# The second product of q and k over all 128 partitions in three attentions

## The chip, the cores and the metric

The kernel runs as one program on one core of a Trainium2 chip. The metric is the device time of one execution in microseconds (us), from the runs of the kernel; a profiled execution beside them gives the trace. A core has five engines that work side by side, each through its own queue in order: TensorE (PE in the rows; its weight loads are listed apart as PEld), VectorE (DVE), ScalarE (ACT), GpSimd (POOL) and SyncE (SP), which issues DMAs. Lines such as L1123 are lines of the kernel before.

## What is computed

Two blocks follow each other on 512 tokens of width 1024, in float32. The first is a hybrid layer: a state-space branch, an attention over a sliding window with sinks, and a mixture of 64 experts. The second puts 16 learned tokens in front (528 rows) and runs two layers, one with a stick-breaking attention and one with a differential attention, each followed by an MLP. Cut to the three products that matter here:

```
scores = einsum('bnqhgd,bnkhd->bnhgqk', qb, kk) * ATT_SCALE      # sliding window: 16 heads of 64, 4 of k
z = einsum('bhqd,bhkd->bhqk', qb, kf) * scale                    # stick-breaking: 16 heads of 64
s = einsum('bhqd,bhkd->bhqk', qb, kk) * scale                    # differential: 8 heads, two q and two k of 64 each
```

In all three the length that is summed over is 64, half of the 128 partitions.

## The kernel before, in words

Matrix products run in a fast format that keeps fewer bits than float32. To keep the accuracy, an operand is split in two: a first part (the rounded value, made by ScalarE with a copy into that format) and a second part (what is left, made by VectorE or GpSimd with a subtraction). A product of two split matrices is then three products that are added into one sum in PSUM: first by first, first by second, second by first (`mm3s`, whose products go through `mm`, L229; where the order of TensorE is pinned to the order of the program they show as L242).

In the attentions the head's length of 64 leaves half of the partitions free, and the kernel uses them: a tile `qs` holds q's first part on 64 partitions and q's second part on the other 64, and `ks` holds k's first part twice. One product of `qs` with `ks` over 128 partitions thus makes two of the three products. The third, q's first part with k's second part `kl`, is made over the 64 partitions on which q's first part stands.

- Sliding window (`swa_qk`, L1080; `swa_scores`, L1107): k of each of the 4 groups stands twice on the partitions already (`kd`, L1049), so `ks` and `kl` are both 128 partitions high. For each group and each of 4 blocks of 128 tokens there are 4 pairs of products, L1122 and L1123, of 256 columns. The steps of this attention are woven with projections of the state-space branch (`dense_x`, `dense_z`), which fill TensorE.
- Stick-breaking (`sb_split`, L1807; `sb_scores`, L1886): two heads share one `kl` tile, the even head on partitions 0 to 63, the odd one on 64 to 127. For each of 16 heads there are products of 512, 384, 256 and 256 columns, L1897 and L1898. Here the order on TensorE is that of the program (`in_order`, L232); `sb_steps` (L1834) writes the stages of the attention out step by step, with the projections of the next heads (`qkv`, L1772) and later of the output (`out_early`, L1738) woven in. `sb_soft` (L1909) and `sb_weights` (L1918) are the work behind the scores: two clippings, exponential, logarithm, and a scan along the keys on VectorE, a subtraction on GpSimd (L1925), an exponential on ScalarE (L1926).
- Differential (`diff_split`, L2341; `diff_scores`, L2355): one `dkl` tile per head holds both second parts, one on each half. For each of 8 heads and 4 blocks of tokens there are 2 pairs of products, and 2 more in the last block; 272, 256, 400, and 256 with 272 columns, L2372 and L2373. The fills are the projections of q, k, v of the later heads and the output projection.

The tiles of these attentions come from pools: `self.la` with tag `qk` (7 buffers) in layer A; the general helper `self.S`, with 34 slots in the second block, in layer B. Which instruction stands where on an engine other than a pinned one is decided by the framework's scheduler; waits and buffer addresses are its work too.

Of the kernel before, what the change touches and what calls it, by code (L numbers as in the profile page):

```python
# [64 lines left out]
class K:  # L65
# [1041 lines left out]
    def swa_scores(self, S, kv, n, mask, snk):  # L1107
        nc, sm = self.nc, self.sm
        k0 = 0 if n else 128
        nk = 256 - k0  # L1110
        x0 = max(n - 1, 0) * 128
        qs = slice(n * 128, (n + 1) * 128)
        ks, kl, qq = S
        pp = []
        for par in range(2):
            p = self.P()
            pp.append(p)
            a = slice(64 * par, 64 * par + 64)
            for i in range(2):
                q = qq[2 * i + par]  # L1120
                o = p[:, i * 256:i * 256 + 256]
                nc.tensor.matmul(o, lhsT=q[:, qs], rhs=ks[:, x0:x0 + 256], start=True, stop=False)  # L1122
                nc.tensor.matmul(o, lhsT=q[a, qs], rhs=kl[a, x0:x0 + 256], start=False, stop=True)  # L1123
        sc = []
        mx = sm.tile([128, 4], F32, tag="mx", bufs=3, name="mx")
        sums = sm.tile([128, 4], F32, tag="sums", bufs=3, name="sums")
        for par in range(2):
            s = self.S(name="sc")
            sv = s[:, :512].rearrange("p (i k) -> p i k", i=2)
            pv = pp[par].rearrange("p (i k) -> p i k", i=2)  # L1130
            for i in range(2):
                nc.vector.tensor_tensor_reduce(sv[:, i, :nk], pv[:, i, :nk], mask[:, k0:], 1.0, NEG, op0=ALU.add, op1=ALU.max, accum_out=mx[:, par * 2 + i:par * 2 + i + 1])
            sc.append(sv)
        sk = snk[:, 4 * kv:4 * kv + 4].rearrange("p (i a) -> p a i", a=2)
        mx2 = mx.rearrange("p (a i) -> p a i", a=2)
        nm = sm.tile([128, 4], F32, tag="nm", bufs=3, name="nm")
        nc.vector.tensor_tensor(mx2, mx2, sk, op=ALU.max)
        es = sm.tile([128, 4], F32, tag="es", bufs=3, name="es")
        nc.vector.tensor_tensor(es.rearrange("p (a i) -> p a i", a=2), sk, mx2, op=ALU.subtract)
        nc.vector.tensor_scalar(nm, mx, -1.0, None, op0=ALU.mult)  # L1140
        nc.scalar.activation(es, es, AF.Exp)
        for par in range(2):
            for i in range(2):
                j = par * 2 + i
                nc.scalar.activation(sc[par][:, i, :nk], sc[par][:, i, :nk], AF.Exp, bias=nm[:, j:j + 1], accum_out=sums[:, j:j + 1])
        nc.vector.tensor_tensor(sums, sums, es, op=ALU.add)
        nc.vector.reciprocal(sums, sums)
        for par in range(2):
            for i in range(2):
                j = par * 2 + i  # L1150
                nc.gpsimd.tensor_scalar(sc[par][:, i, :nk], sc[par][:, i, :nk], sums[:, j:j + 1], None, op0=ALU.mult)
        return (sc,)
# [507 lines left out]
    def layer_a(self, hT, g, g1):  # L1660

        V = self.nc.vector
        h_d = self.H_d("h_d")
        N = self.norm_begin(g, h_d)
        for k in range(8):
            self.norm_tile(N, k, hT[k])
        xs = list(N["xs"])
        self.o_d = self.dr.tile([2, 8, 128, 528], F32, name="o_d")
        r = {}

        def late():
            r["k"], r["c"] = self.norm_end(N, self.KB)
            r["q"] = self.S(name="rq")
            V.tensor_scalar(r["q"], r["k"], 0.125, None, op0=ALU.mult)
        sets = [{"late": False} for _ in range(4)]
        W = self.I["a_w_o"]
        self.ahead([(self.I["a_w_qkv"][i + hg], 2048, 8) for hg in range(4) for i in (0, 4, 8)] + [(W[u][:, :1280], 1280, 5) for u in range(4)]
                   + [(W[u][:, 1280:], 768, 3) for u in range(4)])
        self.rest([self.qkv(0, xs, r, sets[0], late)])
        del hT, N  # L1680
        ho = {}
        heads = [(hg, j) for hg in range(4) for j in range(4)]
        with self.in_order("tensor"):
            fills = [self.qkv(hg, xs, r, sets[hg]) for hg in (1, 2, 3)]
            self.o67 = []
            self.zt = [self.zero_tail(i) for i in range(2)]
            o = [], []

            def loads(k0, k1, to=None):
                for k in range(k0, k1):  # L1690
                    for x, y in zip(o, self.load_o(k, None if to is None else to[2 * k:2 * k + 2])):
                        x.append(y)
                    yield 0.2

            def need(hg, what):
                while what not in sets[hg]:
                    if next(fills[0], None) is None:
                        fills.pop(0)

            def begin(t):  # L1700

                if t == 11:
                    raw = self.st.tile([128, 2112], F32R, tag="raw", bufs=self.NRAW, name="ohl").rearrange("p (a c) -> p a c", a=4)
                    to = [self.hp.tile([128, T2], F32R, tag="h", bufs=8, name="ohl") for _ in range(4)] + [raw[:, x] for x in range(4)]
                    fills.insert(0, loads(0, 4, to))
                if t == 12:
                    fills.insert(0, loads(4, 5))
                if t == 13:
                    self.rest(fills)
                    xs.clear()  # L1710
                    r.clear()
                    fills[:] = [self.out_early(h_d, ho, o)]
                sets[3]["late"] = t >= 14
            self.weave(self.sb_steps(sets, heads, need, begin), fills, .79)
            self.rest(fills)
        o = self.o67
        self.oT = None
        hT = [self.H8() for _ in range(8)]
        self.wide = 2
        N = self.norm_begin(g1)  # L1720
        self.rest([self.out_proj(self.I["a_w_o"], 5, 8, [x[0] for x in o], [x[1] for x in o], ho["h"], self.H, 0, hT, N)])
        self.wide = 0
        return hT, N
# [48 lines left out]
    def qkv(self, hg, xs, r, out, late=None):  # L1772
# [22 lines left out]
        for b, tl in enumerate(self.KB):  # L1795
# [8 lines left out]
                out["v"] = v  # L1804
            yield 1

    def sb_split(self, S, j):  # L1807

        nc = self.nc
        a, o = slice(64 * (j % 2), 64 * (j % 2) + 64), slice(64 - 64 * (j % 2), 128 - 64 * (j % 2))  # L1810
        q, k = S["q"][j // 2], S["k"][j // 2]
        qs, ks = [self.la.tile([128, T2], F32R, tag="qk", bufs=7, name=x) for x in ("qs", "ks")]
        if j % 2 == 0:
            S["kl"] = self.la.tile([128, T2], F32R, tag="qk", bufs=7, name="kl")
        kl = S["kl"]
        S["qk", j] = qs, ks, kl
        nc.scalar.activation(qs[a], q[a], AF.Copy)
        nc.gpsimd.tensor_tensor(qs[o], q[a], qs[a].bitcast(F32), op=ALU.subtract)
# [67 lines left out]
    def sb_scores(self, S, j, tiles):  # L1886


        lo = 64 * (j % 2)
        qs, ks, kl = S["qk", j]  # L1890
        p = self.P()
        c = 0
# [1 line left out]
        for i in tiles:  # L1894
            n, m = 128 * (i + 1), max(128 * (i + 1), 256)
            q = slice(128 * i, 128 * i + 128)
            self.mm(p[:, c:c + m], lhsT=qs[:, q], rhs=ks[:, 0:m], start=True, stop=False)  # L1897
            self.mm(p[:, c:c + m], lhsT=qs[lo:lo + 64, q], rhs=kl[lo:lo + 64, 0:m], start=False, stop=True)  # L1898
            at.append((c, c + n))
            c += n  # L1900
        x = 128 * tiles[-1] if len(tiles) == 1 else 128
# [244 lines left out]
    def layer_b(self, N, bg, kvg, g1):  # L2146
# [56 lines left out]
        def attn():  # L2203
            todo, outs = [], []
            spare = []
            for _ in range(1):
                raw = self.st.tile([128, 2112], F32R, tag="raw", bufs=self.NRAW, name="ohl").rearrange("p (a c) -> p a c", a=4)[:, :, :512]
                spare += [(raw[:, 2 * i], raw[:, 2 * i + 1]) for i in range(2)]
# [17 lines left out]
            for h in range(8):  # L2226
# [5 lines left out]
                for i in range(4):  # L2232
# [6 lines left out]
                    if len(todo) > 3:  # L2239
                        step()  # L2240
                del qk[h]
            while todo:
                step()
                yield 1.5
                norm()
# [95 lines left out]
    def diff_split(self, q, k):  # L2341

        nc = self.nc
        qs, ks = [[self.S(F32R, name=x) for _ in range(2)] for x in ("dqs", "dks")]
        kl = self.S(F32R, name="dkl")
        for m in range(2):
            a, o = slice(64 * m, 64 * m + 64), slice(64 - 64 * m, 128 - 64 * m)
            nc.scalar.activation(qs[m][a, :512], q[a], AF.Copy)
            nc.gpsimd.tensor_tensor(qs[m][o, :512], q[a], qs[m][a, :512].bitcast(F32), op=ALU.subtract)
            nc.scalar.activation(ks[m][a], k[a], AF.Copy)  # L2350
            nc.scalar.activation(ks[m][o], k[a], AF.Copy)
            nc.gpsimd.tensor_tensor(kl[a], k[a], ks[m][a].bitcast(F32), op=ALU.subtract)
        return qs, ks, kl

    def diff_scores(self, h, i, qs, ks, kl, lam):  # L2355
        nc, sm = self.nc, self.sm
# [10 lines left out]
        for x, (a, b) in enumerate(spans):  # L2367
            e = max(b, a + 256)
            for m in range(2):
                lo = 64 * m  # L2370
                p = ps[m, x] = self.P()
                self.mm(p[:, :e - a], lhsT=qs[m][:, i * 128:(i + 1) * 128], rhs=ks[m][:, a:e], start=True, stop=False)  # L2372
                self.mm(p[:, :e - a], lhsT=qs[m][lo:lo + 64, i * 128:(i + 1) * 128], rhs=kl[lo:lo + 64, a:e], start=False, stop=True)  # L2373
            for m in range(2):
                p = ps[m, x]
                if b == L:
# [154 lines left out]
```

## Time and profile before

| | |
|---|---|
| median of 3 runs | 2746.67 us (2743.1 to 2748.12) |
| profiled execution, its own time | 2747.67 us |
| its span, first to last instruction | 2745.9 us |
| mean granted clock of TensorE over the span | 0.977 |
| TensorE busy | 2605.9 us (95%), 18850 products |
| VectorE, ScalarE, GpSimd busy | 1543.9 (56%), 1090.7 (40%), 536.5 us (20%) |

The page gives shares over the whole span; the three attentions take 134, 261 and 223 us of it. A row of a table of instructions has the line, the engine, the operation, out<-in by the program's names, the shapes (for a product: weights' partitions * columns, then the moving operand's partitions x columns), the count, then busy us and mean ns of one, then idle time of the engine before them and what ended it. In a timeline the first number is the start, the second the duration. Starts of products are measured, their ends are modelled: products that follow each other overlap in the rows, so what one costs is read from start to start.

### The profile page before, as it was taken

What the parts mean: (1) busy time and instruction counts of PE and PEld (TensorE: products, weight loads), DVE (VectorE), ACT (ScalarE), POOL (GpSimd) and SP (SyncE); (2) the same over time, 40 slices, a digit from 0 to 9 for tenths busy, and PEclk for the clock granted to TensorE, in tenths of its full rate; (3) what the DMA queues carried; (4) which work ended last, traced back from release to release, by engine and by line L of the source; (5) the groups of instructions that cost most, each with busy time, mean ns of one, the idle gap of its engine ahead of it and who ended that gap; (6) DMA issues with size and microseconds to landing.
All of it is one profiled execution on the core that took longest, in us unless ns stands there. A gap on an engine that the chain in (4) does not pass through costs nothing.

```text
span 2745.9 us, 46828 instructions
## 1 busy us (share of the span) xinstructions
PE 2605.9 (95%) x18850; PEld 2197.3 (80%) x18850; DVE 1543.9 (56%) x3266; ACT 1090.7 (40%) x2249; POOL 536.5 (20%) x528
## 2 busy tenths in 40 slices
PE   7999999999989999996699999999999999999999
PEld 5986769979965555553688889999999777899999
DVE  6488556676652222221688987334467778644433
ACT  5355544433311111111467755323335666523322
POOL 0044332221111011111144430001102435100000
PEclk9999999999999999998799999999999999999999
DMA  5233255544389999994511323222231011322221
GB/s 190 87 123 110 95 182 167 178 142 169 135 363 391 419 416 393 413 413 187 201 55 32 100 80 124 90 83 90 93 128 47 32 55 47 107 86 93 93 93 62
DMA packets 111436, 436.92 MB, mean 159 GB/s; under 512 B 16505, under 2 KB 37545, under 8 KB 68976
## 3 DMA queue, kind: packets, MB, share of 16 engines
q1 hardware_dynamic: 105552, 429.20, 42.6%
q0 software_dynamic: 5520, 4.63, 0.7%
q8 instruction: 150, 2.46, 0.4%
q14 instruction: 70, 0.57, 0.1%
q10 hardware_dynamic: 144, 0.07, 0.0%
HBM read 400.52 MB, written 43.79 MB: 162 GB/s over the span
## 4 chain that ended last, share of the span: by engine, by line
PE 44%; DVE 4%; ACT 2%; issue 1%; POOL 1%; DMA 0%; SPq 0%; DVEq 0%; POOLq 0%; ACTq 0%
PE pd L229 36%; PE pd L242 3%; PE pm L242 2%; PE pm L229 1%; PE pm L2418 1%; DVE zd L1924 1%; DVE wl L180 0%; DVE zd L1913 0%; DVE zt L1912 0%; PE pm L2416 0%; DMA mraw<-y_d 0%; PE pm L2317 0%; ACT wh L179 0%; PE pm L2425 0%; PE pm L2407 0%
## 5 line engine op out<-in xcount | busy, mean ns | idle before, releaser
L229 PE MATMUL pd<-hh,wh 128*128 128x256 f32 (+2 forms) x1408 | 439.1, 313 | 12.5 <-ACT hh L209 8.8
L229 PE MATMUL pd<-hl,wh 128*128 128x256 f32 (+2 forms) x1408 | 438.8, 312 | 1.0 <-DVE hl L210 1.0
L229 PE MATMUL pd<-hh,wl 128*128 128x256 f32 (+2 forms) x1408 | 438.6, 312 | 1.0 <-DVE wl L242 1.0
L206 ACT ACTIVATE wh<-raw 128x1024 fp32r<-128x1024 f32 (+2 forms) x228 | 222.7, 1022 | 413.0 <-PE pd L229 314.2
L207 DVE TENSOR_TENSOR wl<-raw,wh 128x1024 fp32r<-128x1024 f32 (+2 forms) x228 | 281.7, 1266 | 159.4 <-ACT wh L206 159.2
L229 PEld LDWEIGHTS pd<-hh,wh 128*128 128x128 f32 x1408 | 266.9, 190 | 28.4 <-ACT hh L209 9.5
L229 PEld LDWEIGHTS pd<-hh,wl 128*128 128x128 f32 x1408 | 268.1, 191 | 16.7 <-DVE wl L242 1.9
L229 PEld LDWEIGHTS pd<-hl,wh 128*128 128x128 f32 x1408 | 267.8, 190 | 17.1 <-DVE hl L210 1.6
L229 PE MATMUL pd<-wh,hh 128*128 128x256 f32 (+2 forms) x936 | 268.7, 287 | 0.8 <-ACT tk L254 0.5
L229 PE MATMUL pd<-wl,hh 128*128 128x256 f32 (+2 forms) x936 | 264.0, 282 | 0.0
L229 PE MATMUL pd<-wh,hl 128*128 128x256 f32 (+2 forms) x936 | 263.8, 282 | 0.0
L928 PE MATMUL pd<-mraw,xg 128*48 128x256 f32 x2048 | 238.2, 386 | 0.0
L928 PEld LDWEIGHTS pd<-mraw,xg 128*48 128x48 f32 x2048 | 128.7, 124 | 90.1 <-issue 12.7
L229 PEld LDWEIGHTS pd<-wh,hh 128*128 128x128 f32 (+1 forms) x936 | 170.1, 182 | 8.7 <-issue 2.3
L229 PEld LDWEIGHTS pd<-wh,hl 128*128 128x128 f32 (+1 forms) x936 | 169.8, 181 | 2.7 <-issue 0.4
L229 PEld LDWEIGHTS pd<-wl,hh 128*128 128x128 f32 (+1 forms) x936 | 170.2, 182 | 1.9 <-issue 0.2
L898 POOL DMA_INDIRECT y_d<-ys,idx x64 | 60.5, 946 | 475.6 <-DMA y_d<-ys,idx 217.2
L229 PE MATMUL pd<-vl,wh 128*128 128x272 f32 (+1 forms) x512 | 145.3, 285 | 0.0
L229 PE MATMUL pd<-vh,wl 128*128 128x272 f32 (+1 forms) x512 | 145.2, 284 | 0.0
L229 PE MATMUL pd<-vh,wh 128*128 128x272 f32 (+1 forms) x512 | 143.8, 285 | 0.0
L229 PE MATMUL pd<-wh,vh 128*128 128x256 f32 x512 | 142.9, 281 | 0.0
L229 PE MATMUL pd<-wl,vh 128*128 128x256 f32 x512 | 142.8, 281 | 0.0
(572 smaller groups left out, 6286.6 us busy)
## 6 DMA issues: line engine op xcount, KB each, us to landing
mraw<-in_w_moe SPq DMA_DIRECT2D x192, 1024.0 KB, 15.7
raw<-in_mlp_w_in SPq DMA_DIRECT2D x32, 1024.0 KB, 4.9
raw<-in_mlp_w_out SPq DMA_DIRECT2D x32, 1024.0 KB, 4.9
raw<-in_w_xbc SPq DMA_DIRECT2D x12, 1024.0 KB, 5.2
raw<-in_a_w_qkv SPq DMA_DIRECT2D x12, 1024.0 KB, 5.4
raw<-in_w_z SPq DMA_DIRECT2D x8, 1024.0 KB, 5.1
raw<-in_w_gate_in SPq DMA_DIRECT2D x8, 1024.0 KB, 5.3
bc<-acT_d SPq DMA_DIRECT2D x32, 256.0 KB, 5.4
```

What stands on the lines that cost most here:

```text
L206: nc.scalar.activation(h, src, AF.Copy)
L207: nc.vector.tensor_tensor(l, src, h.bitcast(F32), op=ALU.subtract)
L229: self.nc.tensor.matmul(*a, **kw)
L242: return lambda *a, **kw: pin(f(*a, **kw))
L898: self.nc.gpsimd.indirect_dma_start(out=self.y_d[:, :], out_offset=bass.IndirectOffsetOnAxis(ap=rows, axis=0), in_=y[0:64 + self.CAP], in_ ...
L928: self.pin(self.nc.tensor.matmul(p[64 * i:64 * i + self.CAP, 0:256], lhsT=x[:, k], rhs=w[i][:, k], start=k == 0, stop=k == 7))
L1924: nc.vector.tensor_tensor_scan(r[0], r[1], r[0], 0.0, op0=ALU.add, op1=ALU.add)
L2418: nc.tensor.matmul(p[:, 128 * j:512], lhsT=vt[1 + j][h // 4][:, hs], rhs=self.wT[:, j, 128 * j:512], start=False, stop=j == 3)
```

## The change

The second product of each pair runs over all 128 partitions, with the whole `qs` and the whole `kl`. In the sliding window `kl` stands twice, so that product now takes in the product of the two second parts as well. In the other two, `kl` gets zeros on the partitions on which q's second part stands: in layer A two tiles `klz` from a tag of their own, one for even and one for odd heads, while the tag `qk` goes from 7 buffers to 6; in layer B four tiles from the general helper, held through the attention and used in turns of two. The zeros are written once by GpSimd (`kl_tiles`), since each tile always gets its second part on the same half.

```diff
@@ swa_scores
-            a = slice(64 * par, 64 * par + 64)
-                nc.tensor.matmul(o, lhsT=q[a, qs], rhs=kl[a, x0:x0 + 256], start=False, stop=True)
+                nc.tensor.matmul(o, lhsT=q[:, qs], rhs=kl[:, x0:x0 + 256], start=False, stop=True)
@@ layer_a
+        self.klz = self.kl_tiles([self.la.tile([128, T2], F32R, tag="kl", bufs=2, name="klz") for _ in range(2)])
+    def kl_tiles(self, kl):
+        for i, t in enumerate(kl):
+            self.nc.gpsimd.memset(t[64 - 64 * (i % 2):128 - 64 * (i % 2)].bitcast(F32), 0.0)
+        return kl
@@ sb_split
-        qs, ks = [self.la.tile([128, T2], F32R, tag="qk", bufs=7, name=x) for x in ("qs", "ks")]
-        if j % 2 == 0:
-            S["kl"] = self.la.tile([128, T2], F32R, tag="qk", bufs=7, name="kl")
-        kl = S["kl"]
+        qs, ks = [self.la.tile([128, T2], F32R, tag="qk", bufs=6, name=x) for x in ("qs", "ks")]
+        kl = self.klz[j % 2]
@@ sb_scores
-            self.mm(p[:, c:c + m], lhsT=qs[lo:lo + 64, q], rhs=kl[lo:lo + 64, 0:m], start=False, stop=True)
+            self.mm(p[:, c:c + m], lhsT=qs[:, q], rhs=kl[:, 0:m], start=False, stop=True)
@@ layer_b, attn
+            self.klz = self.kl_tiles([self.S(F32R, name="klz") for _ in range(4)])
...
+            self.klz = None
@@ diff_split
-        kl = self.S(F32R, name="dkl")
+        self.kln += 2
+        kl = self.klz[self.kln % 4:self.kln % 4 + 2]
-            nc.gpsimd.tensor_tensor(kl[a], k[a], ks[m][a].bitcast(F32), op=ALU.subtract)
+            nc.gpsimd.tensor_tensor(kl[m][a], k[a], ks[m][a].bitcast(F32), op=ALU.subtract)
@@ diff_scores
-                self.mm(p[:, :e - a], lhsT=qs[m][lo:lo + 64, i * 128:(i + 1) * 128], rhs=kl[lo:lo + 64, a:e], start=False, stop=True)
+                self.mm(p[:, :e - a], lhsT=qs[m][:, i * 128:(i + 1) * 128], rhs=kl[m][:, a:e], start=False, stop=True)
```

## Rows read from the trace of the kernel before

**Rows 1.** The page: the span, and busy time of each engine.

```profile
span 2745.9 us, 46828 instructions
...
PE 2605.9 (95%) x18850; PEld 2197.3 (80%) x18850; DVE 1543.9 (56%) x3266; ACT 1090.7 (40%) x2249; POOL 536.5 (20%) x528
```

**Rows 2.** Stretches: length; PE, PEld, DVE, ACT, POOL busy; clock; DMA share, GB/s.

```profile
231.00:365.00 134.00, 134.00 (x627) 93.33 (x627) 82.41 (x270) 72.43 (x204) 59.89 (x62) 1.00 0.25 85
1379.00:1640.00 261.00, 248.04 (x1775) 214.28 (x1774) 240.33 (x461) 180.27 (x378) 112.51 (x101) 0.99 0.21 65
2112.00:2335.00 223.00, 215.25 (x1306) 168.84 (x1305) 167.94 (x492) 139.93 (x402) 100.53 (x91) 0.95 0.13 41
...
385.00:400.00 15.00, 13.99 (x64) 10.47 (x65) 14.82 (x31) 6.50 (x11) 3.09 (x2) 0.89 0.95 324
790.00:1230.00 440.00, 415.45 (x3094) 242.79 (x3094) 120.31 (x250) 69.79 (x160) 48.30 (x51) 0.99 1.00 408
```

**Rows 3.** Groups by line and shape, PE: all products of 64x columns on kl.

```profile
L1123 PE MATMUL pm<-kl,qs 64*128 64x256 f32 x64 | 24.4, 381 | 0.0
L229 PE MATMUL pm<-dkl,dqs 64*128 64x256 f32 x32 | 12.7, 397 | 0.3 <-POOL dkl L2352 0.3
L229 PE MATMUL pm<-dkl,dqs 64*128 64x272 f32 x32 | 12.6, 395 | 0.0
L242 PE MATMUL pm<-kl,qs 64*128 64x256 f32 x32 | 12.4, 388 | 0.0
L242 PE MATMUL pm<-kl,qs 64*128 64x512 f32 x16 | 8.0, 503 | 0.0
L229 PE MATMUL pm<-dkl,dqs 64*128 64x400 f32 x16 | 7.1, 446 | 0.0
L242 PE MATMUL pm<-kl,qs 64*128 64x384 f32 x16 | 7.0, 438 | 0.0
```

**Rows 4.** Timeline of PE around the first of them: start, duration, instruction.

```profile
230.95 0.28 PE L1122 MATMUL pm<-ks,qs 128*128 128x256 f32 x1
231.16 0.38 PE L1123 MATMUL pm<-kl,qs 64*128 64x256 f32 x1
231.47 0.50 PE L229 MATMUL pd<-hh,wl 128*128 128x512 f32 x1
231.81 0.40 PE L229 MATMUL pd<-hh,wh 128*128 128x512 f32 x1
232.04 0.39 PE L229 MATMUL pd<-hl,wh 128*128 128x512 f32 x1
```

**Rows 5.** Timeline of PE around the last of them, in the differential attention.

```profile
2333.90 0.28 PE L229 MATMUL pd<-ol,wh 128*128 128x256 f32 x1
2334.02 0.29 PE L229 MATMUL pm<-dks,dqs 128*128 128x272 f32 x1
2334.24 0.39 PE L229 MATMUL pm<-dkl,dqs 64*128 64x272 f32 x1
2334.55 0.38 PE L229 MATMUL pd<-oh,wl 128*128 128x256 f32 x1
2334.78 0.40 PE L229 MATMUL pd<-ohl,wh 128*128 128x256 f32 x2
```

**Rows 6.** Timeline of the weight loads, PEld, at the first of them.

```profile
231.16 0.18 PEld L1123 LDWEIGHTS pm<-kl,qs 64*128 64x128 f32 x1 [0.25 <-issue]
...
231.58 0.19 PEld L229 LDWEIGHTS pd<-hh,wh 128*128 128x128 f32 x1
```

**Rows 7.** The chain of waits by line, 1375 to 1640 and 2110 to 2345 us.

```profile
by line: PE pd L242 25.7%; PE pm L242 20.2%; DVE zd L1924 7.8%; issue 5.5%; DVE wl L180 5.0%; DVE zd L1913 5.0%; DVE zt L1912 4.7%; PE pd L229 2.0%; POOL zs L1925 1.8%; DVE zs L1904 1.7%; ACT zs L1926 1.7%; ACT zt L1914 1.7%; ACT wh L179 1.
...
by line: PE pd L229 41.7%; PE pm L229 15.6%; PE pm L2418 9.0%; PE pm L2416 4.3%; PE pm L2407 2.6%; PE pm L2425 2.2%; ACT pr L2386 1.9%; DVE wl L210 1.7%; DVE dmx L2378 1.7%; PE pm L2317 1.4%; DVE wl L207 1.4%; ACT dks L2351 1.4%; issue 1.4%
```

**Rows 8.** POOL: memsets; a wait in 1370 to 1640 us (total, times, longest).

```profile
L666 POOL MEMSET ys<- 128x512 f32 x3 | 1.5, 530 | 0.0
...
POOL kl L1822 <- PE pm L242: 3.1, 2, 1.7
```

More of the change, by code (lines that the diff above doesn't have):

```diff
@@ L1886, in sb_scores @@
     def sb_scores(self, S, j, tiles):
-        lo = 64 * (j % 2)
         qs, ks, kl = S["qk", j]
@@ L2351, in diff_split @@
             nc.scalar.activation(ks[m][o], k[a], AF.Copy)
-            nc.gpsimd.tensor_tensor(kl[a], k[a], ks[m][a].bitcast(F32), op=ALU.subtract)
+            nc.gpsimd.tensor_tensor(kl[m][a], k[a], ks[m][a].bitcast(F32), op=ALU.subtract)
         return qs, ks, kl
+    kln = 0
     def diff_scores(self, h, i, qs, ks, kl, lam):
@@ L2369, in diff_scores @@
             for m in range(2):
-                lo = 64 * m
                 p = ps[m, x] = self.P()
                 self.mm(p[:, :e - a], lhsT=qs[m][:, i * 128:(i + 1) * 128], rhs=ks[m][:, a:e], start=True, stop=False)
-                self.mm(p[:, :e - a], lhsT=qs[m][lo:lo + 64, i * 128:(i + 1) * 128], rhs=kl[lo:lo + 64, a:e], start=False, stop=True)
+                self.mm(p[:, :e - a], lhsT=qs[m][:, i * 128:(i + 1) * 128], rhs=kl[m][:, a:e], start=False, stop=True)
             for m in range(2):
```

## The prediction

> **What bounds the kernel now.** I read the page first: TensorE is busy for 95% of the span, VectorE for 56% [rows 1]. That is an average over stages, so I cut out the three in which the diff edits products, by the first and last start of those products: the sliding-window attention, 231 to 365 us, the stick-breaking attention, 1379 to 1640 us, and the differential attention, 2112 to 2335 us [rows 2]. The first is TensorE's alone: 134.00 busy of 134.00 us, VectorE 82. The third is nearly so: 215 of 223, VectorE 168. In the second VectorE is busy for 240 of 261 us, almost as long as TensorE's 248. Between the first stage and the rest, the stretch 790 to 1230 us is one of DMA (share 1.00); it starts after the work ahead of it, so it can move but not shrink.
>
> Next, the table by shape: how many products does the edit touch, and in which widths? In "64*128 64x256" the first pair is the weights' partitions and columns, the second the moving operand's. The sums are 64 in the first stage, 32+16+16 = 64 in the second and 32+32+16 = 80 in the third: 208 products of 64 partitions [rows 3]. Their durations there (381 to 503 ns) aren't their price, because the ends are modelled and overlap. The price is in the starts, in the timeline.
>
> **The price of one.** The first of the 208: ks starts at 230.95, kl at 231.16, the next product at 231.47, the one after at 231.81, and after that at 232.04 [rows 4]. So: 0.21 from ks to kl, 0.31 from kl to the next, 0.34 from that 512-column product to its successor, where the row pair behind it shows 0.23. A 256-column product of full height needs 0.12, as the one ahead of the last dks shows (2333.90 to 2334.02) [rows 5]. The excess is 0.09 + 0.19 + 0.11 = 0.39 us. The last of the 208 reads the same: 2334.02, 2334.24, 2334.55, 2334.78, which is 0.22, 0.31, 0.23 against 0.12 each: 0.40 [rows 5]. I take 0.39 for each of the 208.
>
> Why does it cost that? The weight loads tell. kl's load starts with its own product at 231.16, after 0.25 us in which the load path was idle and which no wait explains ("issue"), and the next full-height load also comes only behind kl; but the load at 231.58 runs while the product of 231.47 is still under way [rows 6]. A full-height load hides under a full-height product; a change of height is not hidden in either direction, and the queue behind needs one product more to catch up.
>
> **The change, part by part.** *Products.* All 208 become 128 partitions high, with the same columns, weights' columns and count. Beside them stand full-height products of the same shape at 0.12 a piece, so the excess should go: 64 x 0.39 = 25 us in the first stage, 25 in the second, 80 x 0.39 = 31 in the third, 81 in all. That is TensorE's time, not yet the kernel's.
>
> *First stage.* No idle time on TensorE, and the other engines' busy times are far below (VectorE 82 of 134): I take all 25. Ends: 18, if the scores' other work comes late in a quarter of the places, to 27. What was 25 us sooner at 365 stays so: the loads of the DMA stretch go into buffers that the earlier work frees.
>
> *Second stage.* The chain of waits is the view for this. There TensorE's lines hold 25.7 + 20.2 + 2.0 = 48% of the stretch, and VectorE's scans and splits most of the other half [rows 7]. A saving off the chain is worth nothing: 25 x 0.48 = 12. VectorE leaves 261 - 240 = 21 at most, and its pieces take over as TensorE's shrink. I take 9, nearer to the chain's figure than to zero; ends 3 and 21. Late next there is VectorE (zd, zt).
>
> *Third stage.* TensorE holds 41.7 + 15.6 + 9.0 + 4.3 + 2.6 + 2.2 + 1.4 = 77% of the chain [rows 7]: 31 x 0.77 = 24. Ends: 12, if the softmax steps set half of it, to 31.
>
> *What is added.* Six memsets of 64 x 528 or 516 on GpSimd, two at the start of layer A, four at the start of the differential attention. No such shape is in the trace; 128x512 took 530 ns [rows 8], so 6 x 0.53 = 3 us of GpSimd at most, zero at least. It is idle for over half of both stages (112 and 101 busy of 261 and 223) [rows 2], so I cost them at nothing; without that cover the first head's split starts 2 us late in layer B and 1 in layer A. The subtractions that make kl keep their count and shape.
>
> *Tiles.* In layer A kl now alternates between two tiles, and qs and ks have 6 tiles for 4 a pair of heads instead of 7 for 5. The new kl of head j+2 must wait until the scores of head j have read it, which lie a whole head back; the same kind of wait stands in the trace now, 3.1 us in 2 cases [rows 8]. If it lasted longer, the zs subtraction behind it on GpSimd and then ScalarE's exponential would be late. I take zero, ends 0 and 3. In layer B four of the 34 slots of the general helper are held through the attention, where one or two were. No row shows a wait for a slot: zero, with the bad end in the third rival.
>
> *Clock.* Where TensorE runs dry more often, its clock may fall. Over 385 to 400 us, where it has work for 13.99 of 15 us, the granted clock is 0.89, so 15 x 0.22 = 3.3 us at 1.2 in place of 2.4 GHz, 1.7 us of work lost [rows 2]. One or two such stretches more would cost 2 to 3; I leave them in the range.
>
> **Sum.** 25 + 9 + 24 = 58. The profiled execution took 2747.67 us (span 2745.9), 1.0 above the median of the runs, 2746.67. So 2747.67 - 58 = 2690 for it and 2689 for the median. With the low ends 18 + 3 + 12 = 33: 2714, and 2 more for the clock; with the high ends 27 + 21 + 31 = 79: 2668.
>
> **The rivals.** *Everything passes through*: VectorE is released sooner in the second stage too, and the pairs' whole 81 us goes: 2747 - 81 = 2666. For it: TensorE is the chain's largest holder in all three. Against: VectorE's 92% in the second. 0.12.
>
> *Little passes through*: in layer B the four held slots and the softmax steps (mask, maximum, exponential, reciprocal, transposes) set the pace once TensorE no longer does, so that the third stage gains nothing, and the first two only their low ends: 18 + 3 = 21, 2726. For it: 52 and 23% of the two chains [rows 7] are not TensorE's. Against: no slot wait in any view. 0.13.
>
> *The price isn't the height's*: if it came with the data (kl late) or with adding into the same sums, the product would cost the same at full height, and the time stays at 2747. Against: no idle time ahead of kl's 64 products in the first stage [rows 3], and the projections add 24 products into one sum at 0.12. 0.03.
>
> *Slower: the full-height load isn't hidden.* Place: the weight loads of ks, kl and the product behind. If each 0.19 us load [rows 6] stood open ahead of its 0.12, three steps would take 0.93, against 0.21 + 0.31 + 0.22 = 0.74 now: 208 x 0.19 = 40, 2787. It decides from a mean step of 0.25 us on. Against: the load at 231.58 inside the product of 231.47 [rows 6]. 0.04.
> The Trainium skill states that rule ("TensorE: Matmul & The Clock Gate", Part 3, "What overlaps and what doesn't"): a load overlaps products in flight only if it goes to another group of rows. By it a full-height load never hides behind a full-height product, and the change would cost the time just worked out. The trace disagrees: the half-height load waits there, and the full-height one runs ahead.
>
> **How the numbers follow.** The forecast, some 33 to 79 us gained, has 0.68. The range 2667 to 2716 holds it and most of the first rival; out of it lie the three others, 0.20 together. A measurement of this kernel can tell about 0.2%, 5.5 us. Faster: 0.68 + 0.12 + 0.13 = 0.93; same 0.03; slower 0.04.
>
> **What would show it.** Right: in the changed profile no product of 64 partitions is left on kl; ks, kl and the next start 0.12 us apart; the first stage is about 109 us long, the third about 199, and the second shrinks least, with VectorE over 95% busy. Wrong: steps around kl still over 0.2 us (price not the height's); TensorE idle in the third stage for 20 us or more, ended by ScalarE or VectorE on pr (little passes through); the second stage shorter by 20 (VectorE's bound was soft).

## The result, and the profile after

The changed kernel takes 2712.82 us in the median of 4 runs (2708.97 to 2715.8), the kernel before 2746.17 in 4 beside them: a ratio of 0.9877, 95% interval 0.9865 to 0.9888. That is 33 us or 1.2% less, inside the range of the prediction and well clear of the 0.2% that a measurement can tell, but little over half of the 57 that were forecast from the median.

The page of the changed kernel answers [rows 1]:

```profile
span 2707.1 us, 46829 instructions
...
PE 2533.1 (94%) x18850; PEld 2180.6 (81%) x18850; DVE 1546.9 (57%) x3266; ACT 1089.3 (40%) x2249; POOL 537.8 (20%) x534
```

The same number of products, 73 us less of TensorE's busy time, and 39 us less of span (the profiled execution was the fastest of the four). Did the price go? The timeline of TensorE around the first pair, where [rows 4] had steps of 0.21, 0.31 and 0.34:

```profile
230.16 0.39 PE L229 MATMUL pd<-hl,wh 128*128 128x512 f32 x1
230.39 0.28 PE L1121 MATMUL pm<-ks,qs 128*128 128x256 f32 x1
230.51 0.28 PE L1122 MATMUL pm<-kl,qs 128*128 128x256 f32 x1
230.63 0.40 PE L229 MATMUL pd<-hh,wl 128*128 128x512 f32 x1
230.86 0.40 PE L229 MATMUL pd<-hh,wh 128*128 128x512 f32 x1
```

The steps are 0.12, 0.12 and 0.23: kl costs what any product of its width costs. The weight loads of the next pair, beside [rows 6]:

```profile
231.33 0.19 PEld L1121 LDWEIGHTS pm<-ks,qs 128*128 128x128 f32 x1
231.57 0.19 PEld L1122 LDWEIGHTS pm<-kl,qs 128*128 128x128 f32 x1
```

ks starts at 231.56, so kl's load now runs under it. To see where the 39 us come from, cut each stage at the start of its first and of its last ks. First the kernel before at its own marks (columns as in [rows 2], the order of stages third, second, first):

```profile
2112.20:2334.00 221.80, 214.05 (x1299) 167.92 (x1298) 167.38 (x489) 139.73 (x402) 100.53 (x91) 0.95 0.13 42
1379.10:1619.90 240.80, 229.40 (x1628) 196.36 (x1626) 223.81 (x427) 171.35 (x357) 108.88 (x95) 0.99 0.21 67
231.00:364.30 133.30, 133.30 (x624) 92.88 (x622) 82.18 (x268) 72.30 (x204) 59.19 (x61) 1.00 0.25 85
```

Then the changed kernel, first to third:

```profile
230.40:340.90 110.50, 109.87 (x624) 86.73 (x623) 80.29 (x265) 70.15 (x200) 59.02 (x60) 1.00 0.30 103
1353.80:1598.20 244.40, 214.13 (x1626) 197.85 (x1626) 225.46 (x427) 169.11 (x356) 104.22 (x95) 0.96 0.21 66
2090.70:2297.20 206.50, 185.92 (x1292) 159.91 (x1291) 169.41 (x489) 140.08 (x401) 101.73 (x91) 0.96 0.14 45
```

The first stage is 22.8 us shorter, the second 3.6 longer, the third 15.3 shorter: 34.5 in all. What is left of the profile's 39 lies between the stages, 2.6 of it ahead of the second; a difference of that size lies between single executions of one order too (e2_sb and e5_sb_tiles below enter the second stage at 1374.4 and 1378.8 us). So the question is the second and the third stage: TensorE has 15 and 28 us less to do there (229.40 to 214.13, 214.05 to 185.92), and the time did not follow. The chain of waits of the changed kernel, for 1350 to 1618 us, answers to the first row of [rows 7]:

```profile
by line: DVE zd L1927 13.3%; PE pd L242 10.2%; DVE wl L180 10.2%; issue 9.8%; DVE zt L1915 8.5%; DVE zd L1916 6.9%; PE pm L242 4.7%; ACT zt L1917 4.1%; ACT zt L1918 3.5%; DVE zs L1907 2.7%; ACT zs L1929 2.4%; DVE zl L1953 2.3%; DVE wzl L195
```

The TensorE lines shown hold 15% where they held 48%, and VectorE's lines have taken the place.

### The profile page after: what moved, and what is told of

The parts are those of the page before. It is cut to its first block, busy times and chain, and to the rows that moved or that the text cites. A ratio compares the mean times of both kernels' runs of the same rounds, so it can differ in the third digit from the quotient of the medians.

```text
span 2707.1 us, 46829 instructions
## 1 busy us (share of the span) xinstructions
PE 2533.1 (94%) x18850; PEld 2180.6 (81%) x18850; DVE 1546.9 (57%) x3266; ACT 1089.3 (40%) x2249; POOL 537.8 (20%) x534
## 4 chain that ended last, share of the span: by engine, by line
PE 52%; DVE 9%; ACT 3%; DMA 3%; issue 2%; POOL 0%; POOLq 0%; DVEq 0%; ACTq 0%; SPq 0%
PE pd L229 35%; PE pd L928 7%; DMA y_d<-ys,idx 3%; PE pm L787 3%; PE pm L955 3%; DVE zd L1927 1%; PE pd L242 1%; DVE wl L180 1%; DVE zt L1915 1%; DVE zd L1916 1%; PE pm L2425 1%; PE pm L943 1%; PE pm L229 1%; PE pm L242 0%; ACT zt L1917 0%
```

## The experiments

A comparison of two kernels says most if every engine runs its instructions in the same order. The framework's scheduler reorders when tiles change, so I made the pairs that differ in the height alone with the tiles held the same; for those pairs the order of each engine is equal, instruction by instruction. A stage's length is read from one execution of each kernel, so its spread matters. The second stage, where it is that of before, lasts 240.1 to 243.6 us in eight traces (before, e1_swa, e3_diff, e4_swa_diff, e10_diff_tiles, e11_diff_own, e13_nomask_half, e14_nomask_full); the third 218.9 to 221.8 us in four (before, e1_swa, e2_sb, e5_sb_tiles). A difference of 3 us between two single traces thus shows little by itself.

**One stage at a time.** Each of the three edits of the diff alone, and the first and the third together.

> Only the sliding-window attention's second product is made full height. Theory A (the price of 0.39 us a product is all TensorE time in a stage that TensorE alone sets): 64 x 0.39 = 25 us less, 2721. Theory B (what a stage gains is partly lost again in the stages behind it, whose DMA bursts and orders stay): less than 15 us.

> Only the stick-breaking attention: its products full height, with the two zeroed tiles. Theory A (VectorE sets this stage, so TensorE's 25 us are off its chain): 0, between 3 us less and 3 us more. Theory B (the chain share of the forecast): 9 to 12 us less. Theory C (the two alternating tiles and the shorter tag bring a wait on GpSimd that costs time): 3 to 6 us more than before.

> Only the differential attention: full height, with four zeroed tiles held. Theory A (the chain share of the forecast, 77% of 31): 24 us less. Theory B (the softmax steps on VectorE, ScalarE and GpSimd take over once TensorE is faster): 13 to 17 us less, as the trace of the changed kernel shows between its marks.

> The sliding-window and the differential attention full height, the stick-breaking attention as before. Theory A (stick-breaking gives nothing either way): as the changed kernel within 3 us, about 2711. Theory C (there its new tiles cost): 4 us less than the changed kernel, about 2707. By the forecast's share: 9 more than the changed kernel, about 2722.

Beside the kernel before at 2744.63 in these runs: the sliding window alone 2723.24, ratio 0.9921 (0.9904 to 0.9937); the stick-breaking attention alone 2751.27, slower, 1.0024 (1.0013 to 1.0035); the differential attention alone 2729.42, 0.9943 (0.9926 to 0.996); the first and third together 2706.07, 0.986 (0.9843 to 0.9876). For the sliding window the order of all engines is that of before, and its stage is clean:

```profile
230.30:340.80 110.50, 109.91 (x624) 86.74 (x623) 81.10 (x266) 71.42 (x201) 58.99 (x60) 1.00 0.30 103
```

133.3 to 110.5: theory A, 22.8 in place of 25, or 0.36 us a product, and it reaches the end: 21.4 us by the medians. The second edit costs time, 6.6 us by the medians, as theory C had it; whether by that theory's wait on GpSimd is taken up below. The third gains 15, as theory B had it. The first and third together lie 4 to 7 us below the changed kernel (2710.04 and 2712.82 in its two sets of runs), near theory C's 4, though not measured side by side.

**The second stage: height or tiles?** The edit of the stick-breaking attention has two parts. This run keeps the tiles (two zeroed `klz`, tag `qk` with 6) and the old product:

```diff
-            self.mm(p[:, c:c + m], lhsT=qs[:, q], rhs=kl[:, 0:m], start=False, stop=True)
+            self.mm(p[:, c:c + m], lhsT=qs[lo:lo + 64, q], rhs=kl[lo:lo + 64, 0:m], start=False, stop=True)
```

> The stick-breaking attention with its new zeroed tiles and tag sizes, but with the second product still 64 partitions high; the order of every engine is that of e2_sb, so this against e2_sb is the height alone, and this against before the tiles and the order that came with them. Theory A (VectorE sets the stage, the new order is worse, height worth little): slower than before by 5 to 10 us, 2750 to 2755, stage 245 to 250 us between its first and last ks. Theory B (height itself does the harm, by TensorE running dry and its clock falling): as before, 2745, stage 241. Theory C (height is worth its chain share, the order costs more than that): slower than before by 15 or more.

Measured: 2749.72 beside 2745.05, ratio 1.0022 (1.0007 to 1.0038). The stage of this run, tiles without height:

```profile
1378.80:1623.20 244.40, 230.86 (x1626) 197.25 (x1625) 226.08 (x427) 169.61 (x357) 105.77 (x95) 0.98 0.21 66
```

and of the run with both (e2_sb), in the same order:

```profile
1374.40:1618.80 244.40, 214.18 (x1628) 197.81 (x1627) 225.50 (x427) 169.09 (x356) 104.82 (x95) 0.96 0.21 66
```

This pair is the core of the case. The height takes 16.7 us from TensorE (230.86 to 214.18), and the stage is as long (that it agrees to the tenth is chance, by the spread above): all 16.7 became waiting. The medians agree: 2749.72 without the height (beside 2745.05), 2751.27 with it (beside 2744.63). VectorE has 226 of 244 us in both. And the 3.6 us that the stage lost were lost before any height was changed, with the tiles and the order that came with them: all four traces with the new tiles (these two, and two of the changed kernel) take 244.4 to 244.5 us, more than any of the eight above. TensorE's order in this stage is still that of before; in VectorE's, 101 of 427 places hold another instruction. Do the two clippings behind the scores show the loss? In the kernel before from 1379 to 1640 us:

```profile
L1913 DVE TENSOR_SCALAR zd<-zs 128x384 f32<-128x384 f32 (+2 forms) x52 | 35.9, 690 | 0.0
L1912 DVE TENSOR_SCALAR zt<-zs 128x384 f32<-128x384 f32 (+2 forms) x52 | 29.0, 557 | 3.2 <-ACT zs L254 2.2
```

and in the changed kernel from 1353.6 to 1614 us, the same work three lines further down:

```profile
L1915 DVE TENSOR_SCALAR zt<-zs 128x384 f32<-128x384 f32 (+2 forms) x52 | 35.3, 678 | 4.4 <-ACT zs L254 3.4
L1916 DVE TENSOR_SCALAR zd<-zs 128x384 f32<-128x384 f32 (+2 forms) x52 | 32.6, 627 | 0.0
```

Together they take 67.9 us in place of 64.9, but that is no more than a repeat gives: in e1_swa, where this stage has the order of before, they take 67.6 (30.1 and 37.5, 1355.7 to 1616 us). What the means hide is that there are two kinds of clipping. Three lines from the timeline of the kernel before:

```profile
1385.97 1.33 POOL L1925 TENSOR_TENSOR zs<-zs,zd 128x512 f32<-128x512 f32 x1 [19.48 <-DVE zd L1924]
1386.07 1.44 DVE L1913 TENSOR_SCALAR zd<-zs 128x384 f32<-128x384 f32 x1
1505.86 0.35 DVE L1913 TENSOR_SCALAR zd<-zs 128x384 f32<-128x384 f32 x1
```

The first clipping shown ran beside GpSimd's subtraction and ended 0.21 us after it; the second, of the same shape, ran with GpSimd idle and took a quarter of the time. So it is throughout: between the marks of the second stage, a clipping takes 0.39 us in the mean where GpSimd runs nothing beside it, and 0.82 (before) or 0.93 (after) where it does, which is about half of them. VectorE's busy time thus holds waiting. An estimate: what the stage's VectorE instructions took beside GpSimd beyond the mean of the same instruction and shape alone adds up to 42 us in the kernel before and 45 in the changed one. No run took GpSimd's work away, so this is read from times alone.

The wait that theory C named, GpSimd's for the scores that still read kl, grew as well. [rows 8] had 3.1 us in 2 cases; the changed kernel, 1350 to 1618 us, has:

```profile
POOL klz L1826 <- PE pm L242: 8.4, 3, 5.5
```

In e5_sb_tiles it is 7.3 in 4. No wait of TensorE or VectorE between the marks of that run is put down to GpSimd, so it did not hold them directly. Which of the three, the order, the tiles' places or this wait, cost the 3.6 us was not tried.

**The second stage with less for VectorE.** If VectorE is what turns the gain into waiting, the height must be worth something once VectorE has less to do. Both runs leave out the clipping that makes zd, and the scan reads zt in its place; the first has the old height, the second the new.

```diff
-        nc.vector.tensor_scalar(d[:, :n], z[:, :n], 40.0, 0.0, op0=ALU.subtract, op1=ALU.max)
...
-            nc.vector.tensor_tensor_scan(r[0], r[1], r[0], 0.0, op0=ALU.add, op1=ALU.add)
+            nc.vector.tensor_tensor_scan(r[0], r[1], r[1], 0.0, op0=ALU.add, op1=ALU.add)
```

> As e5_sb_tiles, second product 64 high, but the clipping that makes zd (52 instructions of VectorE, 33 to 36 us) is left out and the scan reads zt in both places, so that VectorE has some 205 in place of 240 us of work in the stage. It is the base for e8_noclip_sb, which has the same order. If VectorE sets the stage: shorter than e5_sb_tiles by 10 us or more.

> As e7_noclip_tiles with the second product full height, the order of every engine the same; the zd clipping is left out here too. Theory A (height is worth its 25 us of TensorE wherever VectorE doesn't hold the stage): 15 to 25 us less than e7_noclip_tiles. If the height's gain stays under 5 us here too, VectorE's load isn't what eats it.

Measured as a whole: 2756.19 and 2747.24. Their differential attention, 234 and 231 us long at a granted clock of 0.91 and 0.92, is slower than in any other run, so the stage has to be read by itself. With the old height:

```profile
1373.80:1612.80 239.00, 229.13 (x1628) 197.15 (x1626) 193.69 (x378) 170.89 (x357) 104.61 (x94) 0.98 0.21 67
```

and with the new:

```profile
1376.60:1607.00 230.40, 210.49 (x1628) 196.13 (x1627) 194.12 (x377) 168.56 (x355) 104.63 (x94) 0.96 0.23 70
```

Now the height is worth 8.6 us where it was worth 0.0: VectorE's load is a cause, as far as two pairs of different order can tell. It isn't the whole of it. TensorE got 18.6 us back here and 10 are waiting still, with VectorE at 194 of 230; and taking 32 us from VectorE at the old height shortened the stage by only 5.4, not the 10 that were expected. (At 0.39 us for each of the 52 clippings, only some 20 of the 32 were their own work.) Both theories were half right. A reading that fits, argued and not shown by a run of its own: the stage is a ring of steps through TensorE, VectorE, ScalarE and GpSimd, in which no engine's load alone sets the length. TensorE's longest waits in the second of these runs fit that:

```profile
PE pm L242 <- ACT zs L1930: 9.1, 8, 3.0
PE pm L242 <- DVE wzl L1954: 3.3, 1, 3.3
PE pm L242 <- ACT zs L254: 2.5, 2, 1.5
```

The first is the exponential at the end of the ring, ahead of the transposes of the weights (total us, times, longest).

**The third stage.** The same cut: the four held tiles, with the old height.

```diff
-                self.mm(p[:, :e - a], lhsT=qs[m][:, i * 128:(i + 1) * 128], rhs=kl[m][:, a:e], start=False, stop=True)
+                lo = 64 * m
+                self.mm(p[:, :e - a], lhsT=qs[m][lo:lo + 64, i * 128:(i + 1) * 128], rhs=kl[m][lo:lo + 64, a:e], start=False, stop=True)
```

> The differential attention with its four held tiles, the second product still 64 partitions high. Theory A (tiles and order cost nothing, the softmax steps hold half of TensorE's gain): as before, 2745 within 3, stage 222 us. Theory B (the held slots or the new order cost 8 to 10 us, and the height is worth its 24): 2753 to 2755, stage about 230.

Measured: 2750.4 beside 2745.05, ratio 1.0018 (1.0005 to 1.0031). Its stage:

```profile
2111.90:2335.40 223.50, 211.82 (x1291) 166.07 (x1290) 170.59 (x489) 140.24 (x401) 101.60 (x91) 0.96 0.13 41
```

and with height (e3_diff), in the same order:

```profile
2109.50:2315.90 206.40, 186.19 (x1292) 160.03 (x1291) 169.27 (x489) 140.08 (x401) 101.94 (x91) 0.96 0.14 45
```

The tiles and their order cost the stage 1.7 us (221.8 to 223.5), the height gives 17.1. Both are from single executions; by the medians, each against its base, the tiles cost 5.4 and the height gives 20.6. TensorE has 25.6 us less to do, and its waiting grows from 11.7 to 20.2. Theory A is nearer for the stage; the whole, 2750.4, lies between the two theories, so the tiles are not free. Does VectorE eat the other 8.5? I left out the addition of the mask ahead of the maximum, in both heights, the order again the same in the two:

```diff
-                if b == L:
-                    V.tensor_tensor(p[:, b - a - 128:b - a], p[:, b - a - 128:b - a], mask, op=ALU.add)
```

> As e10_diff_tiles (differential attention, new tiles, second product 64 high), with the mask's addition left out, 64 instructions of VectorE (18 us in the stage). It is the base for e14_nomask_full, whose order is the same. If TensorE alone sets this form: the stage as e10_diff_tiles, 223 us, within 3.

> As e13_nomask_half with full height, the mask's addition left out too. Theory A (VectorE's steps behind the scores eat what the height gives beyond 17 us): the stage is 20 to 28 us shorter than in e13_nomask_half. Theory B (what eats it is not VectorE's load but the order of TensorE's own work and its clock): 17 us again, within 2.

Measured: 2739.0 and 2720.67 beside 2744.44. The stage with the old height:

```profile
2111.40:2324.20 212.80, 206.67 (x1290) 163.79 (x1288) 154.99 (x427) 140.09 (x401) 100.82 (x91) 0.98 0.13 43
```

and with the new:

```profile
2110.90:2304.60 193.70, 181.09 (x1289) 158.29 (x1288) 159.36 (x427) 138.57 (x401) 102.62 (x91) 0.97 0.15 48
```

The height is worth 19.1 here against 17.1, below the 20 to 28 of theory A and at the edge of theory B; by the medians it is 18.3 against 20.6. So these runs don't show that VectorE's mask eats any of the 8.5 us: a difference of 2, with the other sign by the medians, lies within the spread. The stage at the old height became 10.7 us shorter too, against what was expected had TensorE alone set it. But the order changed with it, and some 5 of the 10.7 are TensorE's own busy time (211.82 to 206.67) at a clock of 0.98 in place of 0.96. The waits of TensorE in e3_diff, the longest three of thirteen:

```profile
PE pd L229 <- DVE hT L1767: 2.8, 2, 1.9
PE pd L229 <- DVE vt L2276: 2.6, 2, 1.8
PE pm L2418 <- ACT wm L2419: 2.4, 2, 2.0
```

No one wait holds it. What the rest is, beyond many short waits on VectorE and ScalarE, stays open.

**A version that beats both.** The second stage as before, and two of the four zeroed tiles of layer B out of the general helper's slots:

```diff
-            self.klz = self.kl_tiles([self.S(F32R, name="klz") for _ in range(4)])
+            self.klz = self.kl_tiles([self.wtp.tile([128, T2], F32R, tag="klz", bufs=2, name="klz") for _ in range(2)] + [self.S(F32R, name="klz") for _ in range(2)])
```

> The changed kernel once more, beside e11_diff_own on the same chip: 2713 within 3.

> The sliding-window and the differential attention full height, the stick-breaking attention as before, and two of the four zeroed tiles of layer B moved from the general helper's slots into the pool of wT. If the stick-breaking edit costs 4 to 6 us by its order: 2706 to 2708, below the changed kernel run beside it. If the held slots cost the differential attention time as well: 1 to 3 us less than e4_swa_diff's 2706 and its stage under 206 us; if they don't: as e4_swa_diff.

On one chip: the changed kernel 2710.04 (2708.13 to 2710.55), this one 2703.15 (2699.1 to 2704.05), before 2744.44; ratios to before 0.9869 (0.9839 to 0.99) and 0.9843 (0.9812 to 0.9874). The two sets of runs don't touch, so it is some 7 us better than the changed kernel (which is just inside its 2713 within 3). Its second and third stage:

```profile
1351.60:1593.40 241.80, 231.18 (x1627) 198.84 (x1625) 224.37 (x427) 171.18 (x357) 108.20 (x95) 0.97 0.21 67
2085.80:2289.90 204.10, 187.16 (x1299) 161.33 (x1298) 168.63 (x491) 139.84 (x403) 103.96 (x91) 0.96 0.14 45
```

With all four tiles in the helper's slots the third takes 206.3 to 206.5 us in three traces (e3_diff, and the changed kernel twice) and 209.1 in a fourth (e4_swa_diff):

```profile
2084.50:2293.60 209.10, 188.65 (x1292) 162.09 (x1291) 169.24 (x489) 140.12 (x401) 101.75 (x91) 0.94 0.14 44
```

The fourth ran at a clock of 0.94, and e3_diff has its order, so 209.1 is the exception; against the other three this version is 2 us shorter, from one execution. That is what was expected if the held slots cost time, but the order on TensorE differs a little too, and as a whole, 2703 and 2706, not measured side by side, are no proof that the slots were the cost.

## Why the prediction was right or wrong

**Right: the mechanism and its price.** The price was read from start to start as 0.39 us a product, and laid on the change of height, not on kl's data or the sum. With the order unchanged, the first stage gives 22.8 / 64 = 0.36. The rival that the price isn't the height's is out, and so is the slower one: the full-height load of kl, 0.19 us long, runs under ks, and the steps are 0.12. (In that rival's sum of 0.74 the third step should be 0.23 and not 0.22, which takes some 2 us off its 2787 and changes nothing else.) The rule of the Trainium skill, "TensorE: Matmul & The Clock Gate", Part 3, "What overlaps and what doesn't", by which such a load would stand open, does not hold for these products.

**Right: the first stage.** A stage with no idle time on TensorE and no other engine near its length gave nearly the whole of its price (22.8 of 25), and no loss of it shows in the stretch of DMA behind it: the end of the whole moved with it, 2723.24 against 2744.63.

**Wrong: the second stage, 9 forecast and 3.6 lost.** The step that failed is "25 x 0.48 = 12 ... I take 9, nearer to the chain's figure than to zero". The height is worth nothing there that single traces or medians can tell. The chain's share was used as a price, and it isn't one: it says on which of several nearly equal paths the end lay in one execution, and the pair at equal order shows that here another path, in which VectorE has 226 of 244 us, was as long already. The row that stood beside it, 240 of 261 us on VectorE [rows 2], was given the smaller weight and should have had the larger. A second step failed with it: "I take zero, ends 0 and 3" for the tiles. The tiles and the order that came with them cost 3.6 in the stage, beyond that end. The longer wait on kl that the prediction named did come (8.4 us for 3.1), without being shown to be the cost; a new order on VectorE, ScalarE and GpSimd was not among its terms.

**Mis-sized: the third stage, 24 forecast, 15.3 measured.** The term is "31 x 0.77 = 24": the height gives 17.1, that is 55% of 31 and not 77%, and 1.7 go to the tiles (by the medians 20.6, 66%, and 5.4). The rival "little passes through", which the prediction's paragraph on tiles calls the third though it stands second, named the held slots and the steps of the softmax. The tiles do cost something; what takes the rest of the height's gain stays open.

**The sum.** 22.8 - 3.6 + 15.3 = 34.5 by the marks, 33 by the medians, against 25 + 9 + 24 = 58: the low ends, 18 + 3 + 12 = 33, came out as the sum, though not stage by stage. That the time lies in the range is thus in part luck: the second stage fell below its low end, and the first, near its full value, made up for it.

**What the prediction said it would show.** No product of 64 partitions is left on kl, and the steps are 0.12: yes. First stage about 109: 110.5. Third about 199: 206.5, with TensorE idle for 20.6 of it (206.50 - 185.92). The mark for "little passes through" was 20, ended on pr; in e3_diff, whose third stage is as long, only 4.0 us of TensorE's waits are on pr, so the mark is met in length and not in kind. Second shrinks least with VectorE over 95% busy: it didn't shrink, and VectorE was at 92% (225.46 of 244.40); what kept it there may be a ring of waits, and part of VectorE's 92% is itself waiting for GpSimd.

## What to carry to other kernels

A product of half the height among full-height ones costs more than its columns: fill the other half with zeros, or with a second copy that does no harm, wherever memory allows, and read the gain from start to start. Expect the whole gain only in stages where TensorE has no idle time; where another engine is as busy, take its row before the chain's share, and try the tiles of the edit by themselves, since the tiles and the new order that a scheduler makes for them can cost time of their own. An engine that counts as busy may be held up by another: compare the same instruction beside the other engine's work and alone. A chain of waits gives the place to look, not a price: it tells what was last, not by how much.

## What the runs showed of the hardware beside that

In the second stage, in the same order, the mean granted clock is 0.98 at the old height (e5_sb_tiles) and 0.96 at the new (e2_sb, and the changed kernel twice), while TensorE's waiting went from 13.5 to 30.2 us; over the 244.4 us that is some 0.02 x 244 = 5 us of full-speed time. That the waits brought the lower clock is argued, not tried; with the stage as before it was 0.97 to 0.99 in eight traces. And most of VectorE's instructions that read SBUF alone take longer while GpSimd runs one: in the second stage of the kernel before, the 128x384 clipping that makes zd takes 349 ns in the mean alone (12 of 31) and 1095 beside GpSimd (19), while the subtraction of the same width that reads its product from PSUM (wzl, L1950) takes 543 alone and 542 beside it.
